# More Strassen K pairs in the feed-forward part of a decoder layer: five and eight in the down projection, two in the first block

## The chip, the cores and the metric

One core of a Trainium2 chip runs the whole layer. Its engines are TensorE (PE, matmuls and transposes; PEld is its weight load), VectorE (DVE), ScalarE (ACT), GpSimd (POOL) and SyncE (SP, which issues nearly all loads). The metric is the device time of one execution in microseconds; a run's time is compared by medians.

## The reference

A parallel gated token mixer and then a SwiGLU feed-forward part, on 256 tokens of width 2048 in float32. The change concerns the second:

```python
v = rms_norm(h, norm_ffn[l])
h = h + (jax.nn.silu(v @ w_ffn_gate[l]) * (v @ w_ffn_up[l])) @ w_ffn_down[l]
return rms_norm(h, norm_final)
```

The hidden width is 5632. `w_ffn_gate` and `w_ffn_up` are 2048 x 5632, `w_ffn_down` is 5632 x 2048.

## The kernel before

Every float32 product is made of three matmuls on rounded parts: high x high, high x low, low x high. `wpiece` (L118) loads a piece of a weight matrix (`raw`), ScalarE rounds it to `whi`, VectorE subtracts to get `wlo`. Tokens are the stationary side, in tiles of 128 x 128; the weights are the moving side, 512 columns at a time. Helpers `act`, `tt`, `ts` and `stt` record the operations, so many rows of the profile carry their lines: L57 ScalarE, L60 and L68 VectorE.

**Pairs.** `pair` (L247) multiplies the tokens (two tiles of 128 rows) with two column chunks of 512, `wl` and `wr`, and sums over K, two K tiles (256 rows) at a time. Such a K pair is a 2 x 2 product of blocks. A plain pair takes eight block products, 24 matmuls (all lines L218, through `mm3s`). A pair listed in `skps` goes by Strassen in the Winograd form, with seven products, 21 matmuls: `s_weights` (L222) loads four blocks into `sx`, VectorE makes four sums (`sx`, `se`), ScalarE rounds them (`sh`, `seh`), VectorE subtracts (`sl`, `sel`). The token side needs four sums of 128 x 128 blocks, and their split (`s_sums`, L201; tiles `vsh`, `vsl`). Four of the seven products go to PSUM banks p1, p5, p6, p7, the rest straight into the four result banks q. At the last Strassen pair in the list (`kp == max(skps)`), `u` is made: one ScalarE copy from p1 and three VectorE operations. The list `order` can change the order in which pairs are formed; the last `split` pairs are held back to the end, where their products are made result by result.

**Work that is run later.** The list `later` holds closures: transposes and splits of an earlier result (`to_T`), or `nat_out`, which transposes a block's hidden values into DRAM tiles (`hid`) by eight transposes on TensorE, two ScalarE copies and two POOL DMAs. `run_later` empties it in `pair` at position `late["at"]` (2 here) if no Strassen pair has been met by then, or else behind the last Strassen pair. Its transposes use the banks p1, p5, p7, p6 in turn.

**Stages around the change.** After the output projection, a loop over eleven blocks `f` of 512 hidden columns makes gate and up products with eight K pairs (`FS` = 0, 2, 3, 5 in odd blocks, three pairs in even ones, none in block 0). The tokens' transposes for pairs 4 to 7 are run within block 0. Each block's end is evacuated to `hd`; `nat_out` of it is run in the next block. The down projection then runs in two halves `cc` of 1024 columns, with 22 pairs over the hidden width; `h_of` loads hidden values back from DRAM (`fin`, in three slots), splits them (`ah`, four slots), and makes the sums when the pair goes by Strassen (`DSS`). `at_mid` adds `u` to `hn` there. The buffers: four for `raw`, `whi`, `wlo`; two for `sx`, `sh`, `sl`, `seh`, `sel`; one for `se`; `vsh` and `vsl` hold four pairs. The final norm follows the second half; `own` gives its second token tile banks of its own for the held pairs.

The Tile framework orders the instructions of every engine by its own timeline model, from priorities in program order; the orders of different pairs mix within an engine's queue. Only instructions given to `keep_in_program_order` keep their place.

Of the kernel before, what the change touches and what calls it, by code (L numbers as in the profile page):

```python
# [17 lines left out]
NKT = D // P  # L18
# [11 lines left out]
def hybrid_block_kernel(  # L30
# [13 lines left out]
    w_fg = w_ffn_gate[0]  # L44
    w_fu = w_ffn_up[0]
# [10 lines left out]
    def act(o, i, f=AF.Copy, **kw):  # L56
        return nc.scalar.activation(o, i, f, **kw)  # L57

    def tt(o, a, b, op, eng=None):
        return (eng or nc.vector).tensor_tensor(out=o, in0=a, in1=b, op=op)  # L60
# [9 lines left out]
    late = {"psum": None, "turn": 0, "at": 1}  # L70
# [144 lines left out]
    def mm3s(acc, a, w, first, last, pin=False):  # L215

        for x_, w_, st, sp_ in ((a[0], w[0], first, False), (a[0], w[1], False, False), (a[1], w[0], False, last)):
            m = nc.tensor.matmul(acc, x_, w_, start=st, stop=sp_)  # L218
            if pin:
                tc.keep_in_program_order(m)  # L220

    def s_weights(wl, wr, kp):  # L222
        sx, nb = late["sx"], late["sx_bufs"]
        rows = slice(kp * 2 * P, (kp + 1) * 2 * P)
        x_ = sx.tile([P, 4, 512], F32, tag="sx", name="sx", bufs=nb)
        nc.sync.dma_start(x_[:, 0:2, :], wr[rows, :].rearrange("(k p) n -> p k n", p=P))
        nc.sync.dma_start(x_[:, 2:4, :], wl[rows, :].rearrange("(k p) n -> p k n", p=P))
        e = sx.tile([P, 3, 512], F32, tag="se", name="se", bufs=1)
        h, lo = (sx.tile([P, 4, 512], F32R, tag=t, name=t, bufs=nb) for t in ("sh", "sl"))
        eh, el = (sx.tile([P, 3, 512], F32R, tag=t, name=t, bufs=nb) for t in ("seh", "sel"))  # L230
        tt(e[:, 0, :], x_[:, 0, :], x_[:, 1, :], ALU.add)
        tt(x_[:, 0, :], x_[:, 0, :], x_[:, 2, :], ALU.add)
        tt(e[:, 1, :], x_[:, 0, :], x_[:, 1, :], ALU.add)
        tt(e[:, 2, :], e[:, 1, :], x_[:, 3, :], ALU.add)
        act(h, x_)
        tt(lo, x_, rd(h), ALU.subtract)
        act(eh, e)
        tt(el, e, rd(eh), ALU.subtract)
        t1, r2, l1, l2 = ((h[:, i, :], lo[:, i, :]) for i in range(4))
        t3, t2, t4 = ((eh[:, i, :], el[:, i, :]) for i in range(3))  # L240
        return l1, l2, r2, t1, t2, t3, t4

    def run_later():
        while later:
            later.pop(0)()

    def pair(wl, wr, nkp, skps, a_of, upool=None, split=0, quiet=False, at_mid=None, order=None, own=False):  # L247

        pq = late["psum"]
        qt = [late["acc"].tile([P, 2, 512], F32, tag=f"q{t}", name=f"q{t}") for t in range(2)]
        q = [[qt[t][:, i, :] for i in range(2)] for t in range(2)]
        p = {}
        ns = len(skps)
        left = {(0, 0): 2 * nkp - ns, (0, 1): 2 * nkp - ns, (1, 0): 2 * nkp - ns, (1, 1): 2 * (nkp - ns),
                1: ns, 5: ns, 6: ns, 7: ns}
        begun = set()
        u = None
        if own:  # L260
            left[1, 0], left[1, 1] = left[1, 0] - 2 * split, left[1, 1] - 2 * split
            left[2, 0] = left[2, 1] = 2 * split
            q = q + [[None, None]]

        def go(i, a, w, pin=False):
            left[i] -= 1
            if i in (1, 5, 6, 7) and i not in begun:
                p[i] = pq.tile([P, 512], F32, tag=f"p{i}", name=f"p{i}")
            if i in ((2, 0), (2, 1)) and i not in begun:
                q[2][i[1]] = pq.tile([P, 512], F32, tag=f"p{(1, 5)[i[1]]}", name="last")  # L270
            mm3s(q[i[0]][i[1]] if isinstance(i, tuple) else p[i], a, w, i not in begun, left[i] == 0, pin)
            begun.add(i)

        held = []
        for n_kp, kp in enumerate(order or range(nkp)):
            if n_kp == late["at"] and (not skps or min(skps) > n_kp) and not quiet:
                run_later()
            blk, sums = a_of(kp, kp in skps)
            if kp in skps:
                l1, l2, r2, t1, t2, t3, t4 = s_weights(wl, wr, kp)  # L280
                go(1, blk(0, 0), l1)
                go(5, sums(0), t1)
                go(7, sums(2), t3)
                go(6, sums(1), t2)
                go((0, 0), blk(1, 0), l2)
                go((0, 1), sums(3), r2)
                go((1, 0), blk(1, 1), t4)
                if kp == max(skps):

                    u = upool.tile([P, 4, 512], F32, tag="u", name="u", bufs=1)  # L290
                    act(u[:, 0, :], p[1])
                    tt(u[:, 1, :], u[:, 0, :], p[6], ALU.add)
                    tt(u[:, 2, :], u[:, 1, :], p[7], ALU.add)
                    tt(u[:, 1:4:2, :], p[5].unsqueeze(1).to_broadcast([P, 2, 512]), u[:, 1:3, :], ALU.subtract)
                    if at_mid is not None:
                        at_mid(u)
                    run_later()
                continue
            rows = slice(kp * 2 * P, (kp + 1) * 2 * P)
            ws = [wpiece(w[rows, :], 2, 512) for w in (wl, wr)]  # L300
            todo = [((t, i), [(blk(j, t), (ws[i][0][:, j, :], ws[i][1][:, j, :])) for j in range(2)])
                    for t in range(2) for i in range(2)]
            if kp >= nkp - split:
                held.append(todo)
                continue
            for i, prods in todo:
                for a, w in prods:
                    go(i, a, w)
        for n in range(4):
            for todo in held:  # L310
                i, prods = todo[n]
                if own and i[0] == 1:
                    i = (2, i[1])
                for a, w in prods:
                    go(i, a, w, pin=True)
        return (qt + [q[2]] if own else qt), u
# [72 lines left out]
    for kt in range(NKT):  # L389
# [11 lines left out]
        if kt % 4 in (1, 2):  # L401
            junk = ap_.tile([P, 512], F32, tag="junk", name="junk")
            q, t = kt // 4, kt % 4 - 1
# [408 lines left out]
    for n, cc in ((2, 0), (0, 0), (1, 1), (3, 1), (2, 1), (0, 1)):  # L812
# [4 lines left out]
        q, gate = pair(w_in[:, col:col + 512], w_in[:, col + 512:col + 1024], NKT // 2, GS, u_of, mp,  # L817
                       split=1)
# [26 lines left out]
    fp = ctx.enter_context(tc.tile_pool(name="fp", bufs=1))  # L845
    FS = (0, 2, 3, 5)
# [35 lines left out]
    for cc in range(2):  # L882
        cs = slice(cc * 1024, (cc + 1) * 1024)
        nc.sync.dma_start(hn[:, :, cs], x[:, cs].rearrange("(t p) n -> p t n", p=P))
        q, _ = pair(w_out[:, cc * 1024:cc * 1024 + 512], w_out[:, cc * 1024 + 512:(cc + 1) * 1024], NKT // 2, (),
                    m_of if cc else m_split, split=1)
# [18 lines left out]
    v_of = a_tiles(vth, vtl, FS, vsh, vsl)  # L905
    for f in range(DFF // 512):
        fs = slice(f * 512, (f + 1) * 512)
        q, u = pair(w_fg[:, fs], w_fu[:, fs], NKT // 2, () if f == 0 else FS if f % 2 else (0, 3, 5), v_of, fp, split=1)
        hd = fp.tile([P, 2, 512], F32, tag="hd", name="hd")

        if u is None:
            for t in range(2):
                act(hd[:, t, :], q[t][:, 0, :], AF.Silu, scale=rstd2[:, t:t + 1])
                tt(hd[:, t, :], hd[:, t, :], q[t][:, 1, :], ALU.mult)
        else:
            for t in range(2):
                o = u[:, 2 * t:2 * t + 2, :]
                tt(o, o, q[t], ALU.add)
                act(u[:, 2 * t, :], u[:, 2 * t, :], AF.Silu, scale=rstd2[:, t:t + 1])
            tt(hd, u[:, 0:4:2, :], u[:, 1:4:2, :], ALU.mult)  # L920
        later.append(lambda hd=hd, f=f: nat_out(hd, hid, f"hid{f}_"))
# [7 lines left out]
    nc.gpsimd.dma_start(gfin, norm_final.partition_broadcast(P))  # L929
    ss3 = small.tile([P, 2, 3], F32, name="ss3", bufs=1)  # L930
    ah = uv.tile([P, 4, 2, 2 * S], F32R, tag="tl", name="ah")
    DSS = ((3, 6, 9, 12), (0, 4, 7, 10, 13))

    def h_of(cc, kp, with_sums):
        if cc == 0 and kp < 4:
# [10 lines left out]
        if with_sums:  # L946
            i = (DSS[cc].index(kp) + 2) % len(FS)
            s_sums(v.rearrange("p (a b) -> p a b", a=2), vsh[:, i], vsl[:, i],
# [7 lines left out]
    for cc in range(2):  # L956
        cs = slice(cc * 1024, (cc + 1) * 1024)
        def at_mid(u):
            for t in range(2):
                o = hn[:, t, cs].rearrange("p (a b) -> p a b", a=2)  # L960
                stt(o, u[:, 2 * t:2 * t + 2, :], rstd2[:, t:t + 1], o, ALU.mult, ALU.add)

        q, u = pair(w_fd[:, cc * 1024:cc * 1024 + 512], w_fd[:, cc * 1024 + 512:(cc + 1) * 1024], NFT // 2, DSS[cc],
                    lambda kp, ws: h_of(cc, kp, ws), fp, split=2 if cc else 1, at_mid=at_mid, own=cc == 1)
# [65 lines left out]
```

## Time and profile before

| | us |
|---|---|
| median of 3 runs | 1507.44 |
| lowest, highest | 1506.28, 1512.24 |
| profiled execution, its own time | 1510.63 |
| its span, first to last instruction | 1508.4 |
| output projection, about | 703 to 796 |
| feed-forward blocks 0 to 10, about | 796 to 1262.7 |
| down projection, half 0 and half 1, about | 1262.7 to 1381.2 to 1497.5 |

Times in the rows count from the first instruction. A row of the instruction list gives start, length, engine, line, operation, output <- inputs, shape, number merged and, in brackets, idle time of the engine before it. A matmul's length overlaps its neighbour's, so starts are compared.

### The profile page before, as it was taken

The page shows a single profiled execution, that of the slowest core. Times are in us where ns is not written, and L with a number is a line of the kernel's source. Part 1 is how long each engine was busy: PE and PEld are TensorE (multiplying, and loading weights), DVE is VectorE, ACT ScalarE, POOL GpSimd, SP SyncE. Part 2 cuts the span into 40 slices and gives each one's busy share as a digit, 9 for nine tenths or more (in the row PEclk, how much of TensorE's full clock was granted, in tenths as well). Part 3 has the DMA queues.
Part 4 walks back from the last instruction along what each step waited for, and adds up shares of the span by engine and source line. Part 5 has one row for each costly group of instructions (what it writes and reads, how often), then busy time and mean ns, then how long its engine had stood idle before and what let it go on. Part 6 is the DMA issues. An engine that isn't in the chain of part 4 may idle for free.

```text
span 1508.4 us, 18519 instructions
## 1 busy us (share of the span) xinstructions
PE 1489.2 (99%) x6763; PEld 1225.8 (81%) x6763; DVE 1202.4 (80%) x1400; ACT 821.2 (54%) x944; POOL 71.7 (5%) x94
## 2 busy tenths in 40 slices
PE   8999999999999999999999999999999999999997
PEld 7778888888788888887888888888888888888885
DVE  4756755678898889887568899999989899897865
ACT  5544844555554555544456555555555555655643
POOL 3000300001000000000000000000000000001000
PEclk9999999999999999999999999999999999999999
DMA  7645455556666676656557666576657568786663
GB/s 239 211 150 160 133 187 163 160 187 226 209 210 198 220 261 199 209 191 209 186 180 251 218 216 220 197 237 201 234 179 237 189 223 279 254 279 223 205 213 115
DMA packets 158603, 311.54 MB, mean 207 GB/s; under 512 B 10608, under 2 KB 12720, under 8 KB 158384
## 3 DMA queue, kind: packets, MB, share of 16 engines
q1 hardware_dynamic: 154528, 297.87, 60.4%
q0 software_dynamic: 3952, 12.49, 2.4%
q8 instruction: 53, 0.87, 0.2%
q14 instruction: 38, 0.31, 0.1%
q10 hardware_dynamic: 32, 0.01, 0.0%
HBM read 301.41 MB, written 8.91 MB: 206 GB/s over the span
## 4 chain that ended last, share of the span: by engine, by line
PE 96%; DVE 1%; DMA 1%; issue 1%; ACT 0%; SPq 0%; POOLq 0%; POOL 0%; ACTq 0%; DVEq 0%
PE q L218 61%; PE acc L133 20%; PE p L218 11%; PE ps L165 2%; DMA xq<-in_x_dram 0%; DVE wlo L60 0%; DMA raw<-in_w_in_dram 0%; PE ps L541 0%; PE ps L737 0%; PE ps L560 0%; PE ps L499 0%; ACT whi L57 0%; PE ps L607 0%; PE ps L754 0%; PE ps L693 0%
## 5 line engine op out<-in xcount | busy, mean ns | idle before, releaser
L60 DVE TENSOR_TENSOR wlo<-raw,whi 128x1024 fp32r<-128x1024 f32 (+1 forms) x412 | 504.3, 1230 | 188.7 <-ACT whi L57 186.0
L57 ACT ACTIVATE whi<-raw 128x1024 fp32r<-128x1024 f32 (+1 forms) x412 | 431.7, 1050 | 393.4 <-PE q L218 166.0
L57 ACT ACTIVATE sh<-sx 128x2048 fp32r<-128x2048 f32 x62 | 118.8, 1916 | 116.6 <-PE q L218 41.8
L133 PE MATMUL acc<-wlo,uth 128*128 128x512 f32 (+1 forms) x448 | 173.9, 391 | 0.0
L133 PE MATMUL acc<-whi,utl 128*128 128x512 f32 (+1 forms) x448 | 173.8, 389 | 0.0
L60 DVE TENSOR_TENSOR sl<-sx,sh 128x2048 fp32r<-128x2048 f32 x62 | 141.9, 2289 | 36.1 <-ACT sh L57 36.0
L133 PE MATMUL acc<-whi,uth 128*128 128x512 f32 (+1 forms) x448 | 167.6, 390 | 0.6 <-DVE nat L64 0.4
L218 PE MATMUL q<-wlo,vth 128*128 128x512 f32 x424 | 165.8, 391 | 0.0
L218 PE MATMUL q<-whi,vtl 128*128 128x512 f32 x424 | 165.6, 391 | 0.0
L218 PE MATMUL q<-whi,vth 128*128 128x512 f32 x424 | 164.5, 391 | 0.0
L218 PE MATMUL q<-whi,ah 128*128 128x512 f32 x512 | 159.5, 389 | 0.0
L218 PEld LDWEIGHTS q<-whi,ah 128*128 128x128 f32 x512 | 96.1, 188 | 19.9
L60 DVE TENSOR_TENSOR sel<-se,seh 128x1536 fp32r<-128x1536 f32 x62 | 108.6, 1751 | 4.5 <-ACT seh L57 4.1
L57 ACT ACTIVATE seh<-se 128x1536 fp32r<-128x1536 f32 x62 | 91.7, 1479 | 22.3 <-PE q L218 20.3
L218 PE MATMUL q<-wlo,ah 128*128 128x512 f32 x256 | 99.8, 390 | 0.3 <-DVE wlo L60 0.3
L133 PEld LDWEIGHTS acc<-wlo,uth 128*128 128x128 f32 x448 | 84.8, 189 | 16.9 <-issue 1.0
L133 PEld LDWEIGHTS acc<-whi,utl 128*128 128x128 f32 x448 | 84.8, 189 | 16.5 <-issue 0.7
L133 PEld LDWEIGHTS acc<-whi,uth 128*128 128x128 f32 x448 | 81.7, 188 | 16.9 <-issue 0.7
L218 PE MATMUL q<-wlo,uth 128*128 128x512 f32 x240 | 93.8, 391 | 0.0
L218 PE MATMUL q<-whi,uth 128*128 128x512 f32 x240 | 93.8, 391 | 0.0
L218 PE MATMUL q<-whi,utl 128*128 128x512 f32 x240 | 93.5, 389 | 0.0
L60 DVE TENSOR_TENSOR se<-sx 128x512 f32<-128x512 f32 x124 | 86.2, 695 | 8.8 <-DMA sx<-in_w_in_dram 7.4
(393 smaller groups left out, 2535.6 us busy)
## 6 DMA issues: line engine op xcount, KB each, us to landing
raw<-in_w_in_dram SPq DMA_DIRECT2D x156, 512.0 KB, 3.4
raw<-in_w_ffn_down_dram SPq DMA_DIRECT2D x70, 512.0 KB, 5.1
raw<-in_w_ffn_gate_dram SPq DMA_DIRECT2D x53, 512.0 KB, 4.1
raw<-in_w_ffn_up_dram SPq DMA_DIRECT2D x53, 512.0 KB, 4.8
sx<-in_w_in_dram SPq DMA_DIRECT2D x36, 512.0 KB, 4.3
sx<-in_w_ffn_up_dram SPq DMA_DIRECT2D x35, 512.0 KB, 3.7
sx<-in_w_ffn_gate_dram SPq DMA_DIRECT2D x35, 512.0 KB, 4.7
raw<-in_w_branch_dram SPq DMA_DIRECT2D x32, 512.0 KB, 4.4
```

What stands on the lines that cost most here:

```text
L57: return nc.scalar.activation(o, i, f, **kw)
L60: return (eng or nc.vector).tensor_tensor(out=o, in0=a, in1=b, op=op)
L133: m = nc.tensor.matmul(acc, x_, w_, start=st, stop=sp_)
L165: m = nc.tensor.transpose(pt[:, i * S + t * P:i * S + (t + 1) * P], nat[:, t, (c0 + i) * P:(c0 + i + 1) * P], ident)
L218: m = nc.tensor.matmul(acc, x_, w_, start=st, stop=sp_)
```

## The change

The down projection's two halves get five and eight Strassen pairs, at other places, for four and five. Block 0 gets two (3 and 5), and forms its pairs in the order 0, 1, 2, 4, 3, 6, 5, 7, so these are the fifth and seventh formed. The condition in `pair` now asks whether the first listed Strassen pair is among those formed so far, in the given order; in half 0, whose first is now pair 2, what was put off is run behind pair 14 and no longer at the third pair. Block 0 has a `u` now, and is evacuated as the other blocks are.

```diff
-            if n_kp == late["at"] and (not skps or min(skps) > n_kp) and not quiet:
+            if n_kp == late["at"] and (not skps or skps[0] not in (order or range(nkp))[:n_kp + 1]) and not quiet:
                 run_later()
@@
-        q, u = pair(w_fg[:, fs], w_fu[:, fs], NKT // 2, () if f == 0 else FS if f % 2 else (0, 3, 5), v_of, fp, split=1)
+        q, u = pair(w_fg[:, fs], w_fu[:, fs], NKT // 2, (3, 5) if f == 0 else FS if f % 2 else (0, 3, 5), v_of, fp,
+                    split=1, order=(0, 1, 2, 4, 3, 6, 5, 7) if f == 0 else None)
@@
-    DSS = ((3, 6, 9, 12), (0, 4, 7, 10, 13))
+    DSS = ((2, 5, 8, 11, 14), (0, 2, 5, 7, 10, 12, 15, 17))
```

## Rows read from the trace of the kernel before

**Rows 1.** Page, first section: busy us, share of the span, instructions.
```profile
PE 1489.2 (99%) x6763; PEld 1225.8 (81%) x6763; DVE 1202.4 (80%) x1400; ACT 821.2 (54%) x944; POOL 71.7 (5%) x94
```

**Rows 2.** Waits of TensorE, 796 to 1492 us: total us, times, longest.
```profile
PE q L218 <- DVE wlo L60: 0.3, 1, 0.3
```

**Rows 3.** Chain of waits in order of time, down projection: start, us, what, matmuls merged.
```profile
1313.93 12.92 PE q L218 x57
1326.85 2.72 PE p L218 x12
...
1381.16 2.72 PE p L218 x12
```

**Rows 4.** Instructions of VectorE in order, half 1, an unbroken stretch.
```profile
1410.10 1.02 DVE L60 TENSOR_TENSOR fin<-fin 128x128 f32<-128x128 f32 x4 [2.84 <-DMA fin<-hid]
1411.04 2.28 DVE L60 TENSOR_TENSOR sl<-sx,sh 128x2048 fp32r<-128x2048 f32 x1
1413.25 0.68 DVE L60 TENSOR_TENSOR ah<-fin,ah 128x512 fp32r<-128x512 f32 x1
1413.85 1.75 DVE L60 TENSOR_TENSOR sel<-se,seh 128x1536 fp32r<-128x1536 f32 x1
1415.52 0.68 DVE L60 TENSOR_TENSOR vsl<-fin,vsh 128x512 fp32r<-128x512 f32 x1
1416.12 1.22 DVE L60 TENSOR_TENSOR wlo<-raw,whi 128x1024 fp32r<-128x1024 f32 x1
1417.26 0.68 DVE L60 TENSOR_TENSOR ah<-fin,ah 128x512 fp32r<-128x512 f32 x1
```

**Rows 5.** Groups of instructions, the copy; instructions of VectorE at half 1's u.
```profile
L57 ACT ACTIVATE u<-p 128x512 f32<-128x512 f32 x18 | 10.5, 581 | 0.7 <-PE p L218 0.7
...
1452.34 1.41 DVE L60 TENSOR_TENSOR u<-u,p 128x512 f32<-128x512 f32 x2 [0.45 <-PE p L218]
1453.79 1.22 DVE L60 TENSOR_TENSOR u<-p,u 128x1024 f32<-128x1024 f32 x1
...
1455.53 2.48 DVE L68 SCALAR_TENSOR_TENSOR hn<-u,rstd,hn 128x1024 f32<-128x1024 f32 x2
```

**Rows 6.** Windows of blocks 0 and 1: us, busy us per engine, clock, DMA.
```profile
796.00:842.50 46.50, 46.50 (x214) 38.62 (x214) 40.18 (x51) 29.71 (x35) 0.72 (x1) 1.00 0.77 261
842.50:884.50 42.00, 42.00 (x191) 34.78 (x190) 35.92 (x34) 24.97 (x23) 0.71 (x2) 1.00 0.59 192
```

**Rows 7.** Instructions of SP, PE and DVE in block 0 (three lists).
```profile
796.25 0.37 SPq L226 DMA_DIRECT2D sx<-in_w_ffn_up_dram  x1
...
807.47 1.47 PE L165 MATMUL ps<-ident,hn 128*128 128x128 f32 x12
...
813.47 0.86 DVE L68 SCALAR_TENSOR_TENSOR vtl<-ps,prm,vth 128x256 fp32r<-128x256 f32 x2
...
817.13 0.68 DVE L60 TENSOR_TENSOR se<-sx 128x512 f32<-128x512 f32 x1
```

**Rows 8.** Block 1, its third Strassen pair: VectorE's split, TensorE's first read.
```profile
850.38 2.29 DVE L60 TENSOR_TENSOR sl<-sx,sh 128x2048 fp32r<-128x2048 f32 x1 [1.77 <-ACT sh L57]
...
857.08 0.39 PE L218 MATMUL p<-sl,vth 128*128 128x512 f32 x1
```

**Rows 9.** Start of half 0: VectorE's split of a plain tile, TensorE's first read.
```profile
1272.17 1.22 DVE L60 TENSOR_TENSOR wlo<-raw,whi 128x1024 fp32r<-128x1024 f32 x1
...
1275.36 0.48 PE L218 MATMUL q<-wlo,ah 128*128 128x512 f32 x1
```

**Rows 10.** Half 0, instructions of VectorE: the split for half 1's first pair.
```profile
1319.76 2.28 DVE L60 TENSOR_TENSOR sl<-sx,sh 128x2048 fp32r<-128x2048 f32 x1
```

**Rows 11.** Waits of VectorE, 1381 to 1450 us: total us, times, longest.
```profile
DVE wlo L60 <- ACT whi L57: 7.7, 3, 4.0
DVE fin L60 <- DMA fin<-hid: 5.4, 2, 2.8
```

**Rows 12.** Instructions on the tile hd: landing of its writes to DRAM.
```profile
DMA to landing us min/median/max: 2.5/4.2/8.4
```

## The prediction

> **What bounds the kernel now.** I read the page's first section, then who waited for whom on TensorE from the first feed-forward block to the end of the down projection, then the chain of waits in order of time, then the windows by stage. The page gives matmuls 99% of the span and VectorE 80% [rows 1]. A share alone doesn't say who ends last, so the waits matter: from 796 to 1492 us TensorE waited 0.3 us in all, once, for a split weight tile [rows 2]. The chain gives the real price of a matmul: 57 of them advance the chain by 12.92 us and 12 by 2.72 us, 0.2267 us each [rows 3]; the mean of 390 ns that the page shows for one overlaps its neighbour. So TensorE is full where the change works, at a granted clock of 1.00, the 2.4 GHz level [rows 6], and a removed matmul is worth 0.2267 us until another engine comes last. A pair of K tiles costs 24 matmuls, 5.44 us, plainly and 21, 4.76 us, by Strassen.
>
> The next engine is VectorE. Its price per instruction is the distance from one start to the next in an unbroken stretch [rows 4]: the split of a plain tile (wlo) 1.14 us, of four Strassen blocks (sl) 2.21, of three sums (sel) 1.67, any 128x512 operation (ah, vsl, an addition) 0.60, the four small sums 0.94 together. A plain pair costs VectorE 2 x 1.14 = 2.28 us, a Strassen pair 4 x 0.60 + 2.21 + 1.67 = 6.28. In the down projection either has 0.60 for the hidden tile, and Strassen 0.94 + 0.60 = 1.54 for the sums of the hidden side. So each pair changed takes 0.68 us from TensorE and gives VectorE 4.00 us, or 5.54 in the down projection.
>
> **The change, part by part.** Pairs: 2 more in block 0 (none to two), 1 more in half 0 (four to five), 3 more in half 1 (five to eight). Six pairs x 3 matmuls x 0.2267 = 4.08 us off TensorE. Transposes keep their number. The hidden side's sums for pairs 3 and 5 of block 0 are formed already for the later blocks.
>
> Block 0. VectorE gets 2 x 4.00 = 8.0 us, the combination of u, 1.45 to the start of its last operation and 1.14 for that, which has a wlo's size, 2.6 [rows 5], and an evacuation of three 128x1024 additions (1.14 each, again a wlo's size) in place of two 128x512 ones (0.60), 2.2 more: 12.8 us. In the windows of blocks 0 and 1 it is idle for 46.50 - 40.18 = 6.3 and 42.00 - 35.92 = 6.1 us [rows 6]; TensorE's time shrinks by 1.4. So VectorE is short by 12.8 + 1.4 - 12.4 = 1.8 us over two blocks, and what is split ahead must cover it. The tightest row is the third Strassen pair of block 1: its sl ends at 852.67 and the first matmul that reads it starts at 857.08, 4.4 us later [rows 8]. The Strassen weights can come early, since the loads of the first two are issued at 796.25 and just after, while their additions run after 817 [rows 7]. Bounds: nothing, or, if none of block 0's 6.3 us can be filled, 1.8 + 6.3 - 4.4 = 3.7 us. I take 0.5, near the lower end, because of those early loads.
> The order 0, 1, 2, 4, 3, 6, 5, 7 makes the fourth pair read blocks of the last transposes (807.47, [rows 7]). The last of the eight operations that split them starts near 813.9 [rows 7], TensorE reaches the fourth pair near 807.5 + 1.2 for the transposes + 5.44 = 814.1, and the pair needs only the first four of these, so I put it at nothing; if the evacuation slips by some us, that wait shows at once. The four transposed banks are those that pair 3 writes one plain pair later, with 5 us of cover. At the end only one plain pair, 5.44 us, lies between pair 5 and block 1's first Strassen product, which needs the banks that u reads: one ScalarE copy of 0.58 [rows 5] and 2.6 on VectorE, 3.2. That leaves 2.2, again nothing.
>
> Half 0. The weights of its first Strassen pair can be split in the last block, as now. But pair 2 instead of 3 asks for its sums earlier: 1.54 us on VectorE plus 0.68 that TensorE no longer spends, 2.2, against 2.0 us between the end of a wlo (1273.39) and the first matmul behind it (1275.36) [rows 9]. I take 0.2; the bounds are nothing and 5.54 + 0.68 - 2.0 = 4.2, if the weights too fall into this stretch. Later pairs have more cover: the sl started at 1319.76 [rows 10] belongs to the first pair of half 1, whose 12 matmuls start at 1381.16 [rows 3].
> The move of the last block's output from the third pair to behind pair 14 carries eight transposes, two ScalarE copies and two POOL writes to DRAM. On TensorE they cost the same. Pairs 20 and 21 load what it writes: five plain pairs, 27 us, lie between, the load is asked for three pairs ahead, so 11 us are left, and a write lands after 4.2 us, at most 8.4 [rows 12]. SP would hold this load and the weights behind it until then; POOL has nothing else queued there. Cost nothing; past 11 us each one would be lost in full.
>
> Half 1. VectorE gets 3 x 5.54 = 16.6 us, TensorE loses 2.0. Up to the last Strassen pair, number 17, TensorE has 7 x 4.76 + 10 x 5.44 = 87.7 us. VectorE, with the first two Strassen pairs and pair 1 ready before (as the first is now, [rows 10]), must do six Strassen pairs at 8.42, nine plain ones at 2.88 and 2.5 for half 0's result, two operations like the last of [rows 5]: 78.9 us. Spare 8.8. Against it stand waits in VectorE's own order: for hidden tiles from DRAM 5.4 us in two places, 2.7 each, and for whi 7.7 [rows 11]. Three of the first kind (at pairs 5, 10 and 15, which like those two follow two plain pairs) are 8.1 us and just use up the spare; with all of the second too it is exceeded by 7.0. Many of these waits exist because VectorE now runs ahead. I take 0.5, bounds nothing and 7.0. After pair 17 four plain pairs remain, 21.8 us against 4 x 2.88 + 2.6 + 2.5 of VectorE, so the end of the kernel stays as it is.
>
> The sum: 4.08 - 0.5 - 0.2 - 0.5 = 2.9 us less. The profiled execution took 1510.63 us, 3.2 above the median of 1507.44; on it this gives 1507.7. Against the median, which is what I predict, 1504.5.
>
> **The rivals.** Full gain would be 1507.44 - 4.08 - 0.3 = 1503.1, since 0.3 us is all that TensorE waits there. **Nothing left**: waits of about 4 us, spread over the three places, return 1507.4. For it speaks that spares of 2 us occur in my sums, against it that Strassen splits now end 4.4 us or far more before use. **VectorE comes last in half 1**, the one that ends slower: the dense pairs 10, 12, 15, 17 find neither weights nor sums ready, TensorE waits at each. It decides from 4.1 us of waiting on; at the bound of 7.0 the time is 1510.4, with block 0's 3.7 as well 1514.1, with all three bounds 1518.3. For it speaks that my spare there, 8.8, is no more than the waits seen, 13.1; against it the two early Strassen pairs and that VectorE's waits shrink when it runs less ahead.
> In the window of block 1 weight loads fill 34.78 of 42 us, 83%, and VectorE's instructions 35.92, 86% [rows 6]. The Trainium skill, Perfetto Trace Analysis, "Identifying the Most-Contended Engine", says that matmul busy time is no good measure, to take the weight loads' share for TensorE, and to relieve first the engine with the highest share. By that rule VectorE bounds here already, the change loads the wrong engine, and the time goes to the last rival. The waits row speaks against it, since TensorE's matmuls leave 0.3 us free. **The scheduler** also reorders whole queues after such an edit, and may make or mend small waits anywhere from 796 us on; that moves the time within these bounds.
>
> **How the numbers follow.** The forecast, between full gain and 1506.5: chance 0.66, time 1504.5. Nothing left, 1506.5 to 1508.5: 0.15. VectorE last, above 1508.5: 0.16, of which 0.09 lies above 1515. Below full gain, by something the rows don't show: 0.03. The range for 8 in 10 runs from 1502.8 to 1510.5. A measurement tells about 0.5%, 7.5 us, from no change; the whole of the removed matmuls is 0.27%. So faster by more than that 0.03, within it 0.88, slower 0.09.
>
> **What would show it.** Right: 18 matmuls fewer from 796 us on, at the same 0.2267; TensorE's waits there stay below 1.5 us; VectorE's busy time in half 1 rises by some 16 us with no wait on sl, sel or vsl. Wrong: rows of TensorE waiting for sl, sel, wlo or vsh in block 1, at pair 2 of half 0, or from pair 10 of half 1; SP waiting for the moved write near pair 20; or a chain that goes through VectorE in half 1.

## The result, and the profile after

The changed kernel took 1518.52 us (median of 10 runs, 1516.16 to 1521.16), the kernel before 1511.08 beside it (10 runs, 1506.28 to 1514.51). The ratio of the times is 1.0054, with a 95% interval of 1.0044 to 1.0064 (the quotient of the two medians alone is 1.0049): slower by a small amount that the interval holds clear of no change. The forecast was 2.9 us less, and its range ended at 3.1 us more; what came is some 7 to 8 more. The profiled execution after took 1518.68 us (span 1516.7) against 1510.63 before.

After, first the page's first section (busy us, share, instructions), which answers to [rows 1].

```profile
PE 1490.4 (98%) x6745; PEld 1225.0 (81%) x6745; DVE 1235.4 (81%) x1448; ACT 830.8 (55%) x949; POOL 75.8 (5%) x94
```

There are 18 matmuls fewer, as forecast, and TensorE is busy no less. VectorE does 33 us more. After, the waits of TensorE from 796 to 1510 us (total us, times, longest), which answer to [rows 2].

```profile
PE p L218 <- ACT sh L57: 2.2, 1, 2.2
PE p L218 <- ACT seh L57: 1.7, 2, 1.3
PE p L218 <- issue: 1.7, 1, 1.7
PE q L218 <- DVE u L60: 1.5, 2, 0.8
```

One wait of 0.3 us has become 7.1 us of waits. Most are for rounded weights of a Strassen pair (`sh`, `seh`), which ScalarE makes from VectorE's additions; the 1.7 us put down to "issue" is one more of them, as shown below. The chain of the down projection (start, us, what, matmuls merged) has kept the price of [rows 3], 2.72 us for 12 and 12.92 for 57.

```profile
1443.07 2.72 PE p L218 x12
...
1455.99 12.92 PE q L218 x57
```

So a removed matmul is worth what the prediction said, and time came in elsewhere. To see where, I added up, stage by stage, by how much the distance from one matmul's start to the next exceeds 0.227 us wherever it is over 0.36 us. This counts a wait and also matmuls that run at the lower clock after it. "To the last" is the time from block 0's first matmul to the last one of the down projection. Us; the rows from e1 on are the experiments below.

| kernel | block 0 | block 1 | half 0, with the seam ahead of it | half 1 | sum | to the last | ratio of the times |
|---|---|---|---|---|---|---|---|
| before | 0 | 0 | 0.4 | 0 | 0.4 | 701.0 | 1 |
| after | 4.7 | 5.3 | 0.9 | 0 | 10.9 | 707.9 | 1.0054 |
| e1, block 0 plain | 0 | 0 | 0.6 | 0 | 0.6 | 698.7 | 0.9993 |
| e2, block 0 alone changed | 4.9 | 5.4 | 1.5 | 0 | 11.9 | 711.8 | 1.0067 |
| e3, own temporary | 1.6 | 2.1 | 0.9 | 6.2 | 10.9 | 708.3 | 1.0017 |
| e4, one pair in block 0 | 0 | 5.0 | 2.7 | 0 | 7.6 | 705.7 | 1.0016 |
| e5, one pair fewer in block 1 | 4.8 | 1.0 | 0.6 | 4.8 | 11.1 | 709.2 | 1.0033 |
| e6, e3 and a later multiplication | 2.7 | 2.2 | 1.9 | 0 | 6.8 | 704.8 | 1.0012 |
| e7, e1 and six and nine pairs | 0 | 0 | 0 | 5.8 | 5.8 | 703.5 | 1.0013 |
| e8, e7 and a later multiplication | 0 | 0 | 0 | 4.8 | 4.8 | 702.1 | 1.0024 |
| e9, pairs later in block 0 | 4.4 | 7.5 | 2.2 | 0 | 14.1 | 712.0 | 1.0076 |
| e10, e1 and a later multiplication | 0 | 0 | 0.5 | 0 | 0.5 | 698.8 | 0.9997 |

Blocks 2 to 10 lose nothing in any kernel. After, the account closes to half a microsecond: 4.1 us taken off and 10.9 - 0.4 lost make 6.4; the stretch grew by 6.9. One profiled execution stands behind each row but several runs behind each ratio, and the unchanged code ahead of block 0 ends between 794.1 and 799.6 us, so ratios and sums agree only to some 3 us.

So the time went into blocks 0 and 1, not into the down projection. After, matmuls of block 0 in order (start, us, what; in brackets the idle time before and its releaser).

```profile
820.73 0.39 PE L218 MATMUL q<-whi,vtl 128*128 128x512 f32 x1
822.80 0.47 PE L218 MATMUL p<-sh,vth 128*128 128x512 f32 x1 [1.68 <-issue]
823.11 0.39 PE L218 MATMUL p<-sh,vsh 128*128 128x512 f32 x1
823.34 0.40 PE L218 MATMUL q<-sh,vth 128*128 128x512 f32 x1
825.08 1.22 PE L218 MATMUL p<-seh,vsh 128*128 128x512 f32 x2 [1.34 <-ACT seh L57]
826.10 0.63 PE L218 MATMUL q<-seh,vth 128*128 128x512 f32 x1
826.52 0.63 PE L218 MATMUL p<-sl,vth 128*128 128x512 f32 x1
```

Pair 3's first product was due at 820.73 + 0.23 = 820.96 and starts at 822.80. The profile names no releaser, but the `sh` that it reads ended on ScalarE at 822.71. Three matmuls later TensorE waits again, for `seh`, and then the starts are 0.42 us apart, not 0.227. After, VectorE's instructions in the same place say why.

```profile
816.65 0.68 DVE L60 TENSOR_TENSOR vsl<-s_temp,vsh 128x512 fp32r<-128x512 f32 x1
817.25 1.22 DVE L60 TENSOR_TENSOR wlo<-raw,whi 128x1024 fp32r<-128x1024 f32 x1
818.38 0.69 DVE L60 TENSOR_TENSOR se<-sx 128x512 f32<-128x512 f32 x1
...
822.74 2.29 DVE L60 TENSOR_TENSOR sl<-sx,sh 128x2048 fp32r<-128x2048 f32 x1 [0.35 <-ACT sh L57]
...
826.08 1.75 DVE L60 TENSOR_TENSOR sel<-se,seh 128x1536 fp32r<-128x1536 f32 x1
```

The first weight addition of pair 3 is at 818.38, 2.6 us before its product is due, and behind it come three more additions, the rounding on ScalarE and two subtractions. Its two loads had been issued at 797.53 and 797.95 us. What stood between is `se`: there is one such buffer, and `s_temp`, the temporary for the token sums made in block 0 (L212), takes the same one. Its last reader is the `vsl` at 816.65. Only then can any `se` be written. That was read from the order of the instructions; e3 tests it. Behind the additions ScalarE adds a part of its own: it rounds a plain tile (`whi`, at 819.85 and 822.61) ahead of `sh` and again ahead of `seh`, about 1 us each time. No run tests that order.

From there VectorE has no break over 0.6 us until block 1's third Strassen pair (pair 3), where TensorE waits a second time. After, matmuls of block 1.

```profile
862.06 0.39 PE L218 MATMUL q<-seh,vtl 128*128 128x512 f32 x1
864.66 0.50 PE L218 MATMUL p<-sh,vth 128*128 128x512 f32 x1 [2.21 <-ACT sh L57]
```

After, windows (us, busy us and instructions of PE, PEld, DVE, ACT and POOL, granted clock, DMA share, GB/s): blocks 0 and 1 from the transposes on, the two places of waiting, and half 1. They answer to [rows 6].

```profile
811.50:876.50 65.00, 58.57 (x242) 46.76 (x241) 61.50 (x66) 37.08 (x35) 0.00 (x0) 0.95 0.55 181
817.00:832.00 15.00, 11.97 (x46) 9.16 (x45) 13.88 (x15) 7.87 (x6) 0.00 (x0) 0.89 0.63 211
860.00:870.00 10.00, 7.39 (x26) 5.37 (x25) 9.25 (x10) 3.29 (x2) 0.00 (x0) 0.83 0.66 223
1396.00:1483.00 87.00, 87.00 (x385) 72.06 (x384) 80.83 (x98) 53.30 (x57) 8.20 (x2) 1.00 0.68 222
```

Before, the same two long stretches.

```profile
810.30:875.30 65.00, 65.00 (x289) 53.81 (x288) 57.65 (x63) 39.34 (x38) 0.00 (x0) 1.00 0.64 212
1386.00:1470.00 84.00, 84.00 (x372) 69.60 (x371) 65.41 (x78) 44.84 (x50) 1.86 (x1) 1.00 0.64 206
```

In 65 us of blocks 0 and 1 VectorE is busy for 61.50, and TensorE, full before, is idle for 6.4. In half 1 VectorE is busy for 80.83 of 87 us, nearly as high a share, and TensorE misses nothing. A high share of VectorE alone is not what costs the time.

### The profile page after: what moved, and what is told of

Same layout as the page of the kernel before. It is cut to its first block, busy times and chain, and to the rows that moved or that the text cites. A ratio compares the mean times of both kernels' runs of the same rounds, so it can differ in the third digit from the quotient of the medians.

```text
span 1516.7 us, 18534 instructions
## 1 busy us (share of the span) xinstructions
PE 1490.4 (98%) x6745; PEld 1225.0 (81%) x6745; DVE 1235.4 (81%) x1448; ACT 830.8 (55%) x949; POOL 75.8 (5%) x94
## 4 chain that ended last, share of the span: by engine, by line
PE 94%; DVE 2%; issue 1%; DMA 1%; ACT 1%; SPq 0%; POOLq 0%; POOL 0%; ACTq 0%; DVEq 0%
PE q L218 58%; PE acc L133 20%; PE p L218 12%; PE ps L165 2%; DVE wlo L60 1%; DMA xq<-in_x_dram 0%; DVE u L60 0%; DVE sl L60 0%; DMA raw<-in_w_in_dram 0%; PE ps L541 0%; PE ps L737 0%; ACT whi L57 0%; PE ps L560 0%; PE ps L499 0%; PE ps L607 0%
## 5 line engine op out<-in xcount | busy, mean ns | idle before, releaser
L57 ACT ACTIVATE whi<-raw 128x1024 fp32r<-128x1024 f32 (+1 forms) x400 | 419.1, 1050 | 386.6 <-PE q L218 202.0
L60 DVE TENSOR_TENSOR wlo<-raw,whi 128x1024 fp32r<-128x1024 f32 (+1 forms) x400 | 487.8, 1225 | 173.0 <-ACT whi L57 170.1
L57 ACT ACTIVATE sh<-sx 128x2048 fp32r<-128x2048 f32 x68 | 130.2, 1914 | 97.6 <-DVE sx L60 43.0
L60 DVE TENSOR_TENSOR sl<-sx,sh 128x2048 fp32r<-128x2048 f32 x68 | 155.9, 2293 | 24.3 <-ACT sh L57 24.0
L218 PE MATMUL q<-whi,ah 128*128 128x512 f32 x448 | 140.5, 389 | 0.0
L60 DVE TENSOR_TENSOR sel<-se,seh 128x1536 fp32r<-128x1536 f32 x68 | 119.1, 1751 | 10.3 <-ACT seh L57 10.3
L57 ACT ACTIVATE seh<-se 128x1536 fp32r<-128x1536 f32 x68 | 100.5, 1478 | 44.6 <-DVE se L60 29.0
L60 DVE TENSOR_TENSOR se<-sx 128x512 f32<-128x512 f32 x136 | 94.4, 694 | 9.0 <-DMA sx<-in_w_in_dram 6.9
L218 PEld LDWEIGHTS q<-whi,ah 128*128 128x128 f32 x448 | 84.0, 188 | 17.3
L218 PEld LDWEIGHTS q<-whi,vtl 128*128 128x128 f32 x408 | 76.6, 188 | 15.9
```

## The experiments

**First: which part?** e1 leaves block 0 as before and keeps the down projection's new pairs; e2 does the reverse.

```diff
# e1, against after
-        q, u = pair(..., (3, 5) if f == 0 else FS if f % 2 else (0, 3, 5), v_of, fp,
-                    split=1, order=(0, 1, 2, 4, 3, 6, 5, 7) if f == 0 else None)
+        q, u = pair(..., () if f == 0 else FS if f % 2 else (0, 3, 5), v_of, fp,
+                    split=1, order=None)
# e2, against after
-    DSS = ((2, 5, 8, 11, 14), (0, 2, 5, 7, 10, 12, 15, 17))
+    DSS = ((3, 6, 9, 12), (0, 4, 7, 10, 13))
```

> The changed kernel with block 0 as before (eight plain pairs, no order); the down projection keeps five and eight Strassen pairs. Theory A (all of the loss is made in blocks 0 and 1 by block 0's two Strassen pairs): 4 pairs x 3 matmuls x 0.2267 = 2.7 us less than the kernel before, plus at most the 0.9 us wait at the seam to half 0, ratio 0.998 to 0.999, and no wait of TensorE in block 0 or 1. Theory B (the dense half 1 costs too, hidden in the changed kernel because blocks 0 and 1 came late): ratio at or above 1.000 with waits of TensorE for sl, sel or wlo after 1380 us.

> The changed kernel with the Strassen lists of the down projection as before (four and five), so only block 0 is changed. Theory A: the 10 us of lost TensorE time in blocks 0 and 1 appear as in the changed kernel, 1.4 us of matmuls are saved, so 8 to 10 us slower than before, ratio 1.005 to 1.007. Theory B: no more than half of it, ratio below 1.003.

e1: 1508.62 us, ratio 0.9993 (0.9981 to 1.0004). e2: 1521.55 us, ratio 1.0067 (1.0049 to 1.0085). e1 lies a little above the 0.998 to 0.999 that I had set for it. The whole loss is block 0's: its two pairs alone cost at least as much as both parts together (the intervals overlap). e1's waits of TensorE from 780 to 1515 us, and a window of its half 1:

```profile
PE q L218 <- DVE wlo L60: 0.4, 1, 0.4
```

```profile
1380.00:1467.00 87.00, 87.00 (x386) 72.03 (x385) 84.23 (x103) 54.50 (x60) 8.74 (x2) 1.00 0.69 228
```

The down projection's four pairs alone keep TensorE full, with VectorE busy for 84.23 of 87 us. They shorten the stretch from block 0 on by 701.0 - 698.7 = 2.3 us, where four pairs are worth 2.7. In the time of a whole execution that is 0.15 to 0.18%, and e1's interval neither shows nor excludes it.

**Then: is it the shared buffer, or the load?** Two theories of blocks 0 and 1. By the buffer, pair 3's additions can't use VectorE's idle time before 811 us, because `s_temp` holds `se`. By the load, VectorE simply has too much to do in the two blocks, and the wait moves wherever the buffer lets it. e3 gives `s_temp` a free buffer of another tag and changes nothing else; e4 drops pair 3 and keeps pair 5.

```diff
# e3, against after
-        e = late["sx"].tile([P, 3, 512], F32, tag="se", name="s_temp", bufs=1)
+        e = late["tmp"].tile([P, 2, 512], F32, tag="hd", name="s_temp") if "tmp" in late else late["sx"].tile([P, 3, 512], F32, tag="se", name="s_temp", bufs=1)
-    late["sx"], late["sx_bufs"] = sx, 2
+    late["sx"], late["sx_bufs"], late["tmp"] = sx, 2, fp
# e4, against after
-        q, u = pair(..., (3, 5) if f == 0 else ...
+        q, u = pair(..., (5,) if f == 0 else ...
```

> The changed kernel, but the temporary for the token sums in block 0 takes the idle buffer of hd and not the one buffer of se. Theory A1 (pair 3's four additions start late because se is occupied until the sums of pair 5's tokens are done at 817 us): the additions run near 800 us in VectorE's idle time, the waits of TensorE in blocks 0 and 1 fall from 10 us to under 3, and the time falls to 1 to 4 us below the kernel before, ratio 0.997 to 0.999. Theory A2 (VectorE has too much to do over blocks 0 and 1, wherever it starts): the waits move to block 1 and stay above 6 us, ratio at or above 1.002.

> The changed kernel with one Strassen pair in block 0, number 5, still the seventh formed; pair 3 is plain. Theory A1: pair 5's weights can be split from 817 us on and are due near 835, so block 0 has no wait; block 1 may keep one of 0 to 3 us, because VectorE's 8.8 us more still meet no early idle time; 3.4 us of matmuls are saved: ratio 0.997 to 1.000. Theory A2: about two thirds of the waits stay (8.8 of 12.8 us), ratio 1.002 to 1.004.

e3: 1514.18 us, ratio 1.0017 (1.0004 to 1.0031). Its VectorE in block 0, and further down in half 1:

```profile
801.02 0.69 DVE L60 TENSOR_TENSOR se<-sx 128x512 f32<-128x512 f32 x1 [1.02 <-DMA sx<-in_w_ffn_up_dram]
...
805.17 2.29 DVE L60 TENSOR_TENSOR sl<-sx,sh 128x2048 fp32r<-128x2048 f32 x1
...
808.59 1.75 DVE L60 TENSOR_TENSOR sel<-se,seh 128x1536 fp32r<-128x1536 f32 x1
...
1390.96 5.57 DVE L60 TENSOR_TENSOR ah<-fin,ah 128x512 fp32r<-128x512 f32 x2
```

The additions now start as soon as the load lands, at 801.02 and not 818.38, and pair 3 is split by 810.3 us. The loss in blocks 0 and 1 falls from 10.0 to 3.8 us. The waits of e3's TensorE from 796 to 1510 us:

```profile
PE q L218 <- DVE ah L60: 3.3, 1, 3.3
PE q L218 <- DVE vtl L68: 1.5, 1, 1.5
PE p L218 <- ACT sh L57: 1.3, 1, 1.3
```

So the buffer was the larger part, 6.2 us here (5.1 in e6, which has the same edit), and the expectation "waits below 3 us, no longer slower" was too good: 3.8 us stay (`vtl` in block 0, `sh` in block 1). The last transposes come no later than in after (808.02 and 808.75 us), but VectorE now makes pair 3's splits ahead of the first `vtl`, which starts at 814.26 us and not at 811.57. And a new wait of 3.3 us stands in half 1, for the `ah` above. That one is told of below.

e4: 1513.49 us, ratio 1.0016 (1.0006 to 1.0026). Block 0 loses nothing with one pair, but block 1 still 5.0 us. One pair's 4.00 us on VectorE, and `u`, are enough for the second wait. The 5.0 us are more than the 0 to 3 of theory A1, and the ratio lies between the ranges of the two theories. Waits of e4's TensorE in that stretch:

```profile
PE p L218 <- ACT sh L57: 2.0, 1, 2.0
```

**Is block 1's wait the load?** e5 makes block 1's pair 2 plain, the Strassen pair right ahead of the one that waits. e9 forms block 0's pair 3 one place later, so that its additions have more time; pair 5 stays the seventh formed, and so the two now follow each other, which the expectation doesn't take into account.

```diff
# e5, against after
-        q, u = pair(..., (3, 5) if f == 0 else FS if f % 2 else (0, 3, 5), v_of, fp,
+        q, u = pair(..., (3, 5) if f == 0 else FS if f % 2 and f > 1 else (0, 3, 5), v_of, fp,
# e9, against after
-                    split=1, order=(0, 1, 2, 4, 3, 6, 5, 7) if f == 0 else None)
+                    split=1, order=(0, 1, 2, 4, 6, 3, 5, 7) if f == 0 else None)
```

> The changed kernel with three Strassen pairs (0, 3, 5) in block 1 in place of four; block 0 keeps its two. If the wait of 5.4 us in block 1 comes from VectorE's load over blocks 0 and 1 (theory A2 for that part), it goes away, the 4.9 us of lost time in block 0 stay, and the time is 4 to 5 us below the changed kernel, ratio 1.001 to 1.003. If it comes from the order of buffers in block 1 itself (a late load or a taken buffer), a wait of 4 us or more stays there and the ratio is at or above 1.004.

> The changed kernel with block 0 formed in the order 0, 1, 2, 4, 6, 3, 5, 7: its two Strassen pairs are the sixth and seventh, one plain pair later. Theory A: VectorE works without a break from 811 us until the third Strassen pair of block 1, so the time that block 0 needs not wait for is asked for in block 1 again: 4.9 us of lost time in block 0 fall below 2, that of block 1 stays at 5 us or grows, and the ratio is 1.002 to 1.005. Rival (the place of pair 3 alone is to blame, VectorE has the capacity): both waits fall below 2 us, ratio at or below 1.000.

e5: 1513.99 us, ratio 1.0033 (1.0020 to 1.0047). Block 1's 5.3 us fall to 1.0 and block 0's 4.8 stay, which is the load theory's picture; the ratio lies a little above what I expected, and its trace, of the longest of its ten runs, again has a long `ah` in half 1. By itself e5 doesn't part VectorE's time from the one `se`, which the neighbours 2 and 3 take in turn. The trace of after does: there pair 2's `sel` frees `se` at 859.0 us, and VectorE forms two `wlo` before pair 3's first addition at 861.20. No run gave `se` a second buffer. e9: 1520.04 us, ratio 1.0076 (1.0047 to 1.0105). Waits of e9's TensorE from 796 to 1273 us, the one in block 0, and VectorE's first addition for that pair:

```profile
PE p L218 <- ACT sh L57: 5.5, 3, 2.1
PE p L218 <- ACT seh L57: 2.2, 3, 1.4
...
832.17 0.50 PE L218 MATMUL p<-sh,vth 128*128 128x512 f32 x1 [2.12 <-ACT sh L57]
...
828.76 0.68 DVE L60 TENSOR_TENSOR se<-sx 128x512 f32<-128x512 f32 x1
```

I had expected block 0 below 2 us. It kept 4.4, and block 1 grew from 5.3 to 7.5. But the wait in block 0 is no longer pair 3's, which comes in time: it is that of pair 5, directly behind it, whose additions start at 828.76, behind pair 3's splits and two `wlo`. So one place more was enough for pair 3, and the work only crowded the next pairs. Both theories hold a part: the buffer delays the work (e3), and the delayed work then exceeds VectorE's time up to block 1's third Strassen pair (e4, e5, e9). The second part is argued from these waits and from VectorE's lack of breaks; no run takes away both.

**The new wait in half 1.** In e3 and e5 two `ah` took over 5.5 us in a place where a pair of them takes some 1.3. POOL's instructions in e3 there:

```profile
1390.83 5.16 POOL L60 TENSOR_TENSOR hn<-hn,fin 128x1024 f32<-128x1024 f32 x2 [33.46 <-ACT junk L57]
```

In e5, on VectorE and on POOL:

```profile
1394.87 5.63 DVE L60 TENSOR_TENSOR ah<-fin,ah 128x512 fp32r<-128x512 f32 x2
```

```profile
1394.80 5.16 POOL L60 TENSOR_TENSOR hn<-hn,fin 128x1024 f32<-128x1024 f32 x2 [33.37 <-ACT junk L57]
```

In both, POOL's two multiplications by the final norm's weights (half 0's result) start 0.1 us before the `ah`, and VectorE goes on some 0.5 us after they end. e6 is e3 with these multiplications moved to the end of half 1's accumulation, where few splits are left.

```diff
# e6, against e3
                 # at_mid, behind the stt
+                if cc: tt(hn[:, t, 0:1024], hn[:, t, 0:1024], gfin[:, 0:1024], ALU.mult, nc.gpsimd)
                 # end of half 0
-                tt(o, o, gfin[:, cs], ALU.mult, nc.gpsimd)
```

> Like e3_own_temp, and POOL's two multiplications of half 0's result by the norm weights are moved from the start of half 1 to behind the last Strassen pair of half 1. Theory C (in e3 VectorE's ah at 1391 us took 5 us in place of 0.6 because POOL's 5.2 us multiplications ran in the same moment): no operation of VectorE over 3 us near the start of half 1, the loss of 6.2 us there goes, ratio 0.997 to 0.999 of the kernel before. Rival (ah waited for something else, such as its load): a wait of TensorE over 2 us stays there, ratio at or above 1.001.

e6: 1511.47 us, ratio 1.0012 (1.0000 to 1.0024). The same two `ah` in e6:

```profile
1392.72 1.28 DVE L60 TENSOR_TENSOR ah<-fin,ah 128x512 fp32r<-128x512 f32 x2
```

Half 1 loses nothing now, so the multiplication did hold VectorE. In time e6 can't be told from e3: 6.2 us of half 1 were lost in e3's profiled execution, which at 1518.09 us was the longest of its ten runs (median 1514.18); e5's profiled execution, 1521.09 us, was the longest of its ten as well. How many of the others have that wait is open. Blocks 0 and 1 lose 4.9 us in e6, so it doesn't reach the 0.997 to 0.999 that I had set for it.

**How far the down projection goes.** e7 is e1 with six and nine pairs in the halves, e8 adds e6's later multiplication, e10 is e1 with that multiplication.

```diff
# e7, against e1
-    DSS = ((2, 5, 8, 11, 14), (0, 2, 5, 7, 10, 12, 15, 17))
+    DSS = ((2, 4, 7, 9, 12, 14), (0, 2, 4, 7, 9, 11, 13, 15, 17))
```

> e1_block0_plain with six Strassen pairs in half 0 (2, 4, 7, 9, 12, 14) and nine in half 1 (0, 2, 4, 7, 9, 11, 13, 15, 17). Two more pairs take 1.4 us of matmuls. If VectorE still has cover there (the splits of e1 end 8 to 13 us before use in half 1): no wait over 1 us, 1.4 us below e1, ratio 0.997 to 0.999. If VectorE comes last (my prediction's rival): waits for sl, sel, wlo or vsl in half 0 or 1 of 2 us or more and a time at or above e1's.

> e7_denser_down with POOL's two multiplications of half 0's result moved behind the last Strassen pair of half 1. Theory C: operations of VectorE at the start of half 1 have their usual lengths; if a wait of TensorE stands there in e7, it is gone and the time is lower by it; otherwise the same as e7 within 1 us.

> e1_block0_plain, and POOL's two multiplications of half 0's result are moved behind the last Strassen pair of half 1. e1 has no wait over 0.6 us from block 0 on, so the gain is bounded by its 12 matmuls, 2.7 us: ratio 0.998 to 1.000, no wait of TensorE over 1 us in the down projection. If the move itself costs something at the end (POOL beside the last pairs), a wait on hn after 1470 us and a ratio above 1.000.

e7: 1513.12 us, ratio 1.0013 (1.0003 to 1.0022). e8: 1513.93 us, 1.0024 (1.0013 to 1.0035). e10: 1510.08 us, 0.9997 (0.9987 to 1.0007). Waits of e7's TensorE from 1262 to 1500 us:

```profile
PE p L218 <- DVE sl L60: 1.2, 1, 1.2
PE q L218 <- DVE hn L68: 1.2, 1, 1.2
PE p L218 <- ACT vsh L57: 1.0, 1, 1.0
PE q L218 <- DVE ah L60: 0.9, 1, 0.9
```

The rival "VectorE comes last in half 1" is real, but one pair further on: at nine pairs TensorE waits there for weights, for sums and for a hidden tile in turn, 5.8 us in all, more than the 1.4 us that two further pairs save. The multiplication is at most a small part of that: in e8 4.8 us stay, with the wait for `hn` down to 0.2. No version beat the kernel before by more than its interval; e1 and e10 equal it.

## Why the prediction failed

**The matmul's price held.** 18 fewer, at the same 0.2267 us: in e1, whose other terms are next to nothing, four pairs gave 2.3 of 2.7 us.

**Block 0: the step that failed.** I had VectorE short by 1.8 us over blocks 0 and 1, with bounds of nothing and 3.7, and took 0.5 "because of those early loads". Measured were 4.7 + 5.3 = 10.0 us, beyond the upper bound. Four things were wrong in the step.

- I called block 1's third Strassen pair the tightest row and set no deadline for block 0's own pair 3, where 4.7 of the 10.0 us were lost. By my own figures it was due at 814.1 + 5.44 = 819.5 us, 2.4 us behind the addition of [rows 7] at 817.13. After, it took 4.3 us from its first addition (818.38) to the end of `sh` (822.71).
- An early load is of use only if the next instruction may write its result. [Rows 7] show a load at 796.25 and the first addition at 817.13, and I took the 21 us between for room. It was a wait for the one `se` buffer, which the document had listed. In e3, where that buffer is free, the addition follows 1.02 us of waiting for the load, at 801.02. This is worth 5.1 (e6) to 6.2 (e3) of the 10.0 us.
- I added block 0's idle time, 6.3 us, to block 1's as one stock. Much of block 0's lay ahead of the transposes: there, with `se` held, nothing of the added work could run, and in e3 only pair 3's splits did. From 810 to 875 us the window of before has only 65.00 - 57.65 = 7.4 us of VectorE's idle time, for 12.8 us of new work; after, VectorE worked for 61.50 of 65 us there and was still late. The upper bound did count that block 0's idle time might not be fillable, but it put a lead of 4.4 us [rows 8] against it and priced each us of lateness at one.
- A late pair costs more than its lateness. TensorE waited twice in each place (1.68 and 1.34 us in block 0, 2.21 and 0.40 in block 1), and after it some five matmuls were 0.42 to 0.43 us apart: the granted clock is 0.89 and 0.83 in the two windows, 1.00 before. That makes some 2.7 of the 10.9 us.

The order 0, 1, 2, 4, 3, 6, 5, 7 costs nothing that a row of after shows: no wait on `vtl` stands there. In e3 and e6, where VectorE splits pair 3 first, that wait does show, at 1.5 and 1.6 us. The evacuation through `u`, put at nothing, does cost. The two waits on `u` in after, 1.5 us in all, are these two.

```profile
849.96 0.47 PE L218 MATMUL q<-sh,vth 128*128 128x512 f32 x1 [0.80 <-DVE u L60]
...
1273.94 0.47 PE L218 MATMUL q<-whi,vsh 128*128 128x512 f32 x1 [0.75 <-DVE u L60]
```

The first lies at the start of block 1. The 2.2 us that I had to spare there were for the banks p, and their products came in time (846.28). What was late are the result banks q, which the last additions to `u` read; VectorE, being behind, came to these at 848.60. The second is the seam to half 0, block 10's additions to `u`, which no step of mine spoke of.

**Half 0: 0.2 predicted, 0.9 measured,** all of it at that seam. It isn't the price of pair 2: e2, with the old lists, waits 0.75 us at the same place, and e1, with the new ones, doesn't wait there. VectorE's instructions come in another order around block 10's `u` there, the kind of change that the prediction put down to the scheduler; why they do is open. Pair 2's sums and weights, which I had priced, came in time. The moved output cost nothing in after, as said, but by luck: I had it 11 us ahead of its load. It is transposed at 1359.9 us, 12 us behind pair 14's first products at 1347.5, and SP does wait for it, which I had named as a sign of being wrong. After, waits of SP from 1340 to 1391 us:

```profile
SPq L940 <- DMA hid<-hd: 3.5, 2, 1.9
```

TensorE had enough split ahead not to notice. In the other kernels with this list for half 0 (e1, e3 to e6, e9, e10) it lost 0.5 to 2.1 us in the plain pairs behind pair 14, to waits for `wlo` (before lost 0.4 there, behind its pair 12), so half 0 is not as free as after alone shows.

**Half 1: 0.5 predicted, nothing measured.** The bound of 7.0 supposed that VectorE keeps its waits for `whi` and `fin`; the prediction also said that many of them exist because VectorE runs ahead. The second was right. VectorE's waits from 1391 to 1482 us after, against [rows 11]:

```profile
DVE wlo L60 <- ACT whi L57: 3.5, 1, 3.5
DVE sl L60 <- ACT sh L57: 2.5, 3, 1.8
```

The two waits for `fin` are gone and those for `whi` are down from 7.7 us to 3.5. The splits are done early: the six `sl` made in half 1 end 9.5 to 15.4 us before the first product that reads them. Busy time rose from 65.41 in 84 us to 80.83 in 87, about the 16 us that I had named as the sign of being right.

**The rivals and the chances.** The slower rival was put in the wrong stage: it needed the price of blocks 0 and 1, and I gave that 0.5 us. "Above 1508.5" had a chance of 0.16, and slower by more than 0.5% one of 0.09; the measured 0.54% stands on that line, and its interval contains it. The Trainium skill, Perfetto Trace Analysis, "Identifying the Most-Contended Engine", takes the engine with the highest share for the bound. In blocks 0 and 1 the time went its way. In half 1 it did not: VectorE at 80.83 of 87 us, in e1 at 84.23, and TensorE missed nothing. What told the two stages apart was not the share but how long ahead the splits could be made: 9.5 us and more in half 1, nothing in block 0.

## What to carry to other kernels

Before idle time of an engine is counted as room, ask of each added operation from when on it may run: its input loaded, and the buffer that it writes free, also from another tile of the same tag; a long distance between a load and its first use is as likely a wait as a choice. Sum spare time only from that moment to the moment of use, not over whole stages. And price a late operand at more than its lateness: the clock may fall with the wait, as it did in blocks 0 and 1 here, though not after every wait of this size.

## What the runs showed of the hardware that I had not expected

**POOL's multiplications held VectorE.** Beside POOL's 128x1024 multiplications, two `ah` of VectorE took 5.57 us (e3) and 5.63 us (e5), and 1.28 without (e6). Taken singly, each `ah` of e3 ended 0.55 us after the POOL instruction that had begun before it. All operands of both are in SBUF. The Trainium skill, SBUF — State Buffer, "Who interferes with whom", says that a VectorE instruction with two SBUF inputs contends with a GpSimd instruction that reads SBUF, by an exclusive lock on the port pair that they share, and that the order of issue decides who is blocked. These rows agree, as far as VectorE starting after POOL goes. In after the same multiplications took 8.64 us from 1395.56 on, where an `ah` of VectorE was still running, while a `wlo` at 1395.70 took its usual 1.22 and one `ah` at 1401.86 2.89: there POOL seems to have been the one held, though spans on POOL are rough. Before, a `wlo` beside them took 3.42 us. So this cost was there all along and hidden; TensorE paid for it plainly where a hidden tile was due (3.3 us in e3, 3.2 in e5).

**The clock fell after some waits and not after others of like size.** After, two gaps of 1.68 and 1.34 us with three matmuls between left the granted clock at 0.89 from 817 to 832 us. In e3 a single gap of 1.49 us stands at 818.70, and the clock didn't fall; a longer single one, 3.3 us, took it down. It is not the two pieces that decide: e9 has two gaps of 1.59 and 1.36 us in block 1, again with three matmuls between, and the clock stayed at 1.00 up to 862 us. What decides is open. Windows of e3 (two), then the place in e9 and its window:

```profile
817.00:832.00 15.00, 13.52 (x60) 11.01 (x60) 14.86 (x19) 7.75 (x9) 0.00 (x0) 1.00 0.69 227
1390.00:1404.00 14.00, 10.70 (x36) 8.30 (x35) 13.05 (x9) 7.33 (x10) 5.16 (x2) 0.76 0.54 154
...
856.56 0.50 PE L218 MATMUL p<-sh,vth 128*128 128x512 f32 x1 [1.59 <-ACT sh L57]
...
858.88 0.73 PE L218 MATMUL p<-seh,vsh 128*128 128x512 f32 x2 [1.36 <-ACT seh L57]
...
852.00:862.00 10.00, 7.05 (x30) 5.08 (x29) 9.26 (x9) 5.18 (x4) 0.00 (x0) 1.00 0.55 158
```

Behind the 3.3 us some twelve matmuls ran at 0.43 us distance, the 1.2 GHz level, which made 3.3 us of waiting 6.2 us of loss.
